# Ten instead of seven up-projection pairs in seven products, three in a row with a plain one between; half of a low part by VectorE where two of them meet

## The chip, the cores and the metric

One core of a Trainium2 chip runs the whole layer in one launch. The metric is the device time of one execution in microseconds. The kernel before takes 816.15 us (median of 3 runs, 815.88 to 816.3).

## The reference

One layer of a bidirectional encoder over 512 tokens of width 1024: attention and a gated scan side by side, cross-attention into 256 memory rows, and a gated MLP with a depthwise convolution of three taps between the up-projection and the activation. The change is in the MLP (and one copy in the scan).

```python
def conv_ffn(h, w_up, conv_w, conv_b, w_down):        # h 512 x 1024, w_up 1024 x 5632
    u = h @ w_up
    half = CONV_W // 2                                # CONV_W = 3
    up = jnp.pad(u, ((0, 0), (half, half), (0, 0)))
    acc = conv_b
    for j in range(CONV_W):
        acc = acc + up[:, j:j + n] * conv_w[j]
    gate, val = jnp.split(acc, 2, axis=-1)            # 2816 columns each
    return (jax.nn.silu(gate) * val) @ w_down

def reference(x, mem, ...):
    ...
    mixed = jnp.concatenate([att, rec], axis=-1) @ w_out[l]
    x = x + rmsnorm(mixed, post_mix_g[l])
    ...
    x = x + rmsnorm(memory_cross_attention(h, m, w_xq[l], w_xkv[l], w_xo[l]), post_x_g[l])
    h = rmsnorm(x, pre_ffn_g[l])
    x = x + rmsnorm(conv_ffn(h, w_up[l], conv_w[l], conv_b[l], w_down[l]), post_ffn_g[l])
    return x
```

## The kernel before, in words

**Arithmetic.** A float32 number is split into a high part and a low part (the number minus its high part), both in a rounded type that TensorE multiplies fast. Each product is three matmuls (`mm3`): high by high, high by low, low by high. On the page these are L278, L279 and L280. PE names the matmul, PEld the load of its stationary operand, which is here the block of weights. So L280's load needs the low part of the weights and the other two need the high part.

**Up-projections.** `w_up` is cut into 22 up-projections, i = 0 to 21, each with 128 columns of the gate and 128 of the value. An up-projection is done in one of two ways:

- *plain:* two units of weights, 1024 rows x 128 columns each, one for the gate and one for the value. A unit is laid out as 128 partitions x 1024 and takes 24 matmuls of 512 columns.
- *a pair in seven products* (`strassen_pair`, the i in `UP_S`): gate and value together, by Strassen's scheme in Winograd's form, with seven products of half size instead of eight. The products are w11, w22, t2, w21, t3, t1, t4 in this order, each with four steps of `mm3`, 84 matmuls of 256 columns in all. The weights are four units: **diag** (w11 and w22, from DRAM), **side** (t2 and w21, where w21 comes from DRAM and t2 is summed on the chip), **sums** (t3 and t1, a tile called "both") and **last** (t4, half the size). VectorE sums blocks for them in `add_blocks`: L197 writes "both" from the raw diag and the raw side, L200 writes t2 over the first half of the raw side, and the sum for t4 follows. Before the change the pairs are 6, 8, ..., 18, with a plain one between any two of them.

**A unit's way** (`issue`, called with three units in hand, `AHEAD`): SP loads the raw block from DRAM by DMA (L189, 512 KB). ACT casts the high part `wh` (L222). The low part `wl` is made in one of two ways. Either VectorE subtracts (L224), or ACT writes the negated high part into `wl` (L229) and a DMA from POOL's queue adds the weights from DRAM to it (L230). `LOW_FROM` says from which column on the second way is used: the diag wholly (512 KB by DMA), the side from column 512 on (256 KB; its first half isn't in DRAM), all others not at all. `wh` and `wl` have four buffers each, so a unit takes those of the unit four before it and waits until TensorE is done with them. The raw blocks have two rooms called "raw" and two called "tmp", in turn.

**Sums for the down-projection.** It uses the same scheme, with sums of blocks of `w_down` kept in DRAM. They are made beside the up-projections: a DMA from SP copies a block (a seed), and a DMA from POOL's queue adds another one (L251, an *add*, 512 KB; the last of each six has 256 KB). An add is issued behind a mark, a tiny copy on POOL (L236) that waits for the low part of the unit just issued. `adds_at` holds the units that are followed by an add. Each plain up-projection from 2 on gives one, and a second one only where no pair stands ahead of it.

**After the products** come the convolution (`conv`: one step on ACT, L1069, and two on VectorE, L1070, for each of gate and value), the activation, and the product of gate and value (L1083). For a pair, VectorE also joins the seven results out of PSUM (L1146 to L1155). Each engine works off its own instructions in order; how the four engines' instructions are interleaved in each queue is decided by a scheduler when the program is built, from the code's order and its data dependencies.

**The scan** (`hgrn_core`, four heads) copies two operands at L632, `kc` and `qc`. The copy of `qc` for head 1 is on VectorE and all others are on ACT.

Of the kernel before, what the change touches and what calls it, by code (L numbers as in the profile page):

```python
# [20 lines left out]
T = 512  # L21
# [4 lines left out]
FF = 2816  # L26
NF = FF // P
EPS = 1e-6
UP_S = (6, 8, 10, 12, 14, 16, 18)
N_MIX, N_WHOLE = 66, 110 - 2 * len(UP_S)  # L30
N_DOWN = N_WHOLE + 4 * len(UP_S)
N_UNITS = N_DOWN + 42
# [5 lines left out]
UP_PRODUCTS = (("w11", 0), ("w22", 1), ("t2", 0), ("w21", 1), ("t3", 1), ("t1", 0), ("t4", 0))  # L38
LAY_AHEAD, LOAD_AHEAD = 3, (7, 5)
SIDES_AT = (19, 20)  # L40
LOW_FROM = {"diag": 0, "side": 512}
SEEDS_AT = frozenset(range(28, 46)) | frozenset(range(60, 66))
ADDS_AT = frozenset(range(56, 62))
NEG_GROUP = frozenset((p, 1) for p in (2, 5, 6))
# [3 lines left out]
NEG_SCALAR = frozenset(range(9, 33))  # L48
NEG_POOL = frozenset(range(33, 42))
# [9 lines left out]
def pat(t, off, dims):  # L59
    a = t[:]  # L60
    return bass.AP(tensor=a.tensor, offset=a.offset + off, ap=[list(a.ap[0])] + [list(d) for d in dims])
# [28 lines left out]
def layer(tc, io, out):  # L90
    nc = tc.nc
# [16 lines left out]
    def bank(tag):  # L108
        return ps.tile([P, 512], F32, name="ps_" + tag, tag=tag)
# [35 lines left out]
    plan = [("w", i) for i in range(N_MIX)]  # L145
    whole, adds_at = N_MIX, set(ADDS_AT)
    for i in range(NF):
        if i in UP_S:
            plan += [(kind, UP_S.index(i)) for kind in ("diag", "side", "sums", "last")]
        else:  # L150
            if i >= 2:
                adds_at.update((len(plan), len(plan) + (i - 1 not in UP_S)))
            plan += [("w", whole), ("w", whole + 1)]
            whole += 2
    assert len(plan) == N_DOWN and whole == N_WHOLE
# [16 lines left out]
    def source(i):  # L172
        kind, n = plan[i]
        return io["w"][n] if kind == "w" else io["wu"][n, ("diag", "side").index(kind)]

    def load_w():
        i = loaded[0]
        loaded[0] += 1
        if i >= N_DOWN:
            p, u = divmod(i - N_DOWN, 6)  # L180
            cols = width(u)
            raw = raw_room(i)[:, :cols.stop - cols.start]
            src = weight_block(PRODUCTS[p][0], cols)
        else:
            if plan[i][0] in ("sums", "last"):
                return None
            raw = raw_room(i)
            src = source(i)
        last_load[0] = nc.sync.dma_start(raw, src).ins  # L189
        return raw  # L190

    def add_blocks(kind, raw, ahead):
        if kind == "diag":
            both = vp.tile([P, 1024], F32, name="both", tag="vv")
            mid = ahead[:, :512]
            with tc.issue_after(last_low[0]):
                nc.vector.tensor_tensor(out=both.rearrange("p (a n) -> p a n", a=2),  # L197
                                        in0=raw.rearrange("p (a n) -> p a n", a=2),
                                        in1=mid[:, None, :].to_broadcast([P, 2, 512]), op=ALU.add)
            nc.vector.tensor_add(mid, both[:, :512], raw[:, half(1)])  # L200
            pair_sums["sums"] = both
        elif kind == "side":
            pair_sums["last"] = tmp2(tag="tq")
            nc.vector.tensor_add(pair_sums["last"], raw[:, :512], raw[:, half(1)])
# [3 lines left out]
    def issue():  # L208
        i = issued[0]
        issued[0] += 1  # L210
        raw = raws.popleft() if raws else load_w()
        kind = plan[i][0] if i < N_DOWN else "w"
        if kind == "diag" and not raws:
            raws.append(load_w())
        if raw is None:
            raw = pair_sums[kind]
        wh = wp.tile([P, 1024], F32R, name="wh", tag="wh")
        wl = wp.tile([P, 1024], F32R, name="wl", tag="wl")
        if raw.shape[1] < 1024:
            wh, wl = wh[:, :raw.shape[1]], wl[:, :raw.shape[1]]  # L220
        by_dma = 0 if i in NEG_SCALAR or i in NEG_POOL else LOW_FROM.get(kind, raw.shape[1])
        nc.scalar.copy(wh, raw)  # L222
        if by_dma:
            last_low[0] = nc.vector.tensor_sub(wl[:, :by_dma], raw[:, :by_dma], wh[:, :by_dma].bitcast(F32)).ins  # L224
        if by_dma < raw.shape[1]:
            if i in NEG_POOL:
                nc.gpsimd.tensor_scalar(wl, wh.bitcast(F32), -1.0, 0.0, op0=ALU.mult, op1=ALU.add)
            else:
                nc.scalar.mul(wl[:, by_dma:], wh[:, by_dma:].bitcast(F32), -1.0)  # L229
            nc.gpsimd.dma_start(wl[:, by_dma:], source(i)[:, by_dma:], accum_op=ALU.add)  # L230
        add_blocks(kind, raw, raws[0] if raws else None)
        pending.append((wh, wl))
        if i in SEEDS_AT:
            seeds.popleft()()
        if i in adds_at and adds:
            with tc.issue_after(nc.gpsimd.tensor_copy(mark, wl[:, 0:1].bitcast(F32)).ins):  # L236
                adds.popleft()()
# [22 lines left out]
    def issue_ahead():  # L260
        while issued[0] < min(hold[0], taken[0] + AHEAD):
            issue()
        while N_MIX + 4 <= taken[0] and loaded[0] < min(N_UNITS, taken[0] + LOAD_AHEAD[loaded[0] >= N_DOWN]):
            raws.append(load_w())
# [189 lines left out]
    raw = rawp.tile([P, 1024], F32, name="raw", tag="raw")  # L454
# [163 lines left out]
    def hgrn_core(h):  # L618
        while h not in heads:
            yield None  # L620
        q, qk, tt = heads[h]
# [4 lines left out]
        diag = a[:, :, 0, :]  # L626
# [2 lines left out]
        nc.vector.scalar_tensor_tensor(out=ksum, in0=qk[:, 1, 1, :], scalar=oml[:, 1, h:h + 1], in1=ksum,  # L629
                                       op0=ALU.mult, op1=ALU.add)  # L630
        for side, to in ((1, kc), (0, qc)):
            (nc.vector.tensor_copy if (h, side) == (1, 0) else nc.scalar.copy)(  # L632
                to, pat(qk, side * 2 * T, [[2, T // 2], [T + 1, 2]]))
        o = bank("c").rearrange("p (b n) -> p b n", b=NB)
        for b in range(NB):
            nc.tensor.matmul(o[:, b, :], ksum[:, blk(b)], q[:, blk(b)], start=True, stop=True)
# [197 lines left out]
    def cores():  # L834
        for h in range(3):
            yield from hgrn_core(h)
# [94 lines left out]
    def attention_filler():  # L931
# [11 lines left out]
        kv["y0"] = yield from res_first(mix, MIX_ORDER, lambda j: rec_done[0] == 4 if j >= 2 else att_done[0] >= 2 * j + 2)  # L943

    weave((hgrn_core(3), 22.0), (attention(), 46.0), (attention_filler(), 52.0))

    x = load_x()
# [180 lines left out]
    def strassen_pair(i):  # L1128
        g, m, n = next_bank(), next_bank(), next_bank()
        place = {"w11": (g, near), "t2": (m, far), "t1": (m, near), "w22": (n, near), "t3": (n, far),  # L1130
                 "w21": (g, near), "t4": (g, far)}
        two, more, val = tmp2(tag="th"), tmp2(tag="th"), tmp2(tag="tq")
        for k, (name, at_w) in enumerate(UP_PRODUCTS):
            if k % 2 == 0:
                w = take()
            (hi, lo), cols = left_h[name]
            o, at = place[name]
            o = o[:, at]
            for kc in range(4):
                wc = slice(at_w * 512 + kc * P, at_w * 512 + kc * P + P)  # L1140
                mm3(o, (w[0][:, wc], w[1][:, wc]), (hi[:, kc, cols], lo[:, kc, cols]), kc == 0 and name != "w21",
                    kc == 3, name == "w21")
            if name == "w11":
                nc.scalar.copy(two[:, near], o)
            elif name == "t2":
                nc.vector.tensor_sub(two[:, far], o, two[:, near])  # L1146
            elif name == "t3":
                nc.vector.tensor_add(more[:, far], o, two[:, far])
            elif name == "t1":
                nc.vector.tensor_add(more[:, near], o, two[:, far])  # L1150
                nc.vector.tensor_tensor(out=val.rearrange("p (a t) -> p a t", a=2),
                                        in0=n.rearrange("p (a t) -> p a t", a=2),
                                        in1=more[:, None, near].to_broadcast([P, 2, 256]), op=ALU.add)
            elif name == "t4":
                nc.vector.tensor_sub(o, o, more[:, far])  # L1155
        conv(0, i, g)
        conv(1, i, val)

    for i in range(2, NF):
        if i in UP_S:  # L1160
            strassen_pair(i)
# [185 lines left out]
```

## Time and profile before

| what | value |
|---|---|
| runs, median (lowest to highest) | 816.15 us (815.88 to 816.3) |
| the profiled execution | 816.71 us |
| its span, first to last instruction | 813.8 us |
| granted TensorE clock, mean | 0.998 |
| up-projections in pairs, plain | 7, 15 |
| L222, casts of weights (ACT) | 110, 113.7 us |
| L224, low parts by VectorE | 77, 92.3 us |

The span is shorter than the time because the time also has the start and the end of the program. In the views below a row of a timeline is start, duration (us), engine, line, operation and tiles, then the idle time ahead of it and what ended that. A row of the DMA view is tiles, queue, count, KB each and the median time from issue to landing. A row of windows is the stretch, its length, and for each engine the busy time and number of instructions, then the clock, the busy share of the DMA engines and GB/s.

### The profile page before, as it was taken

To read this page: it belongs to the slowest core of one execution; us is meant where nothing else is said; L and a number is where in the kernel's file an instruction comes from. 1 tells how busy PE (TensorE), PEld (TensorE's weight loads), DVE (VectorE), ACT (ScalarE), POOL (GpSimd) and SP (SyncE) were. 2 spreads that over 40 slices of the span, in tenths; PEclk is the share of its full clock that TensorE was granted. 3 is DMA by queue.
4 is the path that set the end of the run, shared out by engine and by line. 5 is a ranking of instruction groups with operands and counts; after the bars stand their busy time and mean duration, and the time that the engine had idled before them with its cause. 6 is when DMAs were issued, how large, how long until landed. Compare 5 with 4: busy or idle time off the path is not lost.

```text
span 813.8 us, 11771 instructions
## 1 busy us (share of the span) xinstructions
PE 803.3 (99%) x4426; PEld 691.0 (85%) x4426; DVE 574.7 (71%) x868; ACT 482.1 (59%) x796; POOL 136.9 (17%) x213
## 2 busy tenths in 40 slices
PE   9999999999999999999999999999999999999996
PEld 7888888889998887888888898899999998888885
DVE  5456587469886865855453767987777788888765
ACT  5675757459988874644543553665555545566651
POOL 0111201053233102301010311211111111000301
PEclk9999999999999999999999999999999999999999
DMA  8685645569899753256634158776665677278852
GB/s 296 202 259 139 160 103 117 118 159 247 229 250 254 182 172 126 78 181 157 180 117 142 33 164 208 154 200 166 179 171 143 150 200 178 91 208 278 239 130 104
DMA packets 42457, 139.61 MB, mean 172 GB/s; under 512 B 5280, under 2 KB 6560, under 8 KB 42400
## 3 DMA queue, kind: packets, MB, share of 16 engines
q1 hardware_dynamic: 28944, 97.43, 35.5%
q0 software_dynamic: 12160, 38.54, 26.2%
q10 hardware_dynamic: 1296, 2.89, 1.0%
q8 instruction: 34, 0.56, 0.3%
q14 instruction: 23, 0.19, 0.1%
HBM read 135.17 MB, written 25.17 MB: 197 GB/s over the span
## 4 chain that ended last, share of the span: by engine, by line
PE 92%; DVE 3%; ACT 2%; issue 1%; POOL 1%; DMA 0%; DVEq 0%; POOLq 0%; SPq 0%; ACTq 0%
PE ps_b L279 10%; PE ps_b L280 10%; PE ps_b L278 10%; PE ps_s L278 6%; PE ps_s L280 6%; PE ps_s L279 6%; PE ps_o L278 5%; PE ps_o L279 5%; PE ps_o L280 5%; PE ps_c L278 5%; PE ps_c L280 5%; PE ps_c L279 5%; PE ps_c L647 3%; PE ps_o L893 2%; PE ps_s L872 2%; PE ps_o L882 2%
## 5 line engine op out<-in xcount | busy, mean ns | idle before, releaser
L222 ACT CAST wh<-raw 128x1024 fp32r<-128x1024 f32 x110 | 113.7, 1035 | 114.6 <-PE ps_b L279 35.3
L224 DVE TENSOR_TENSOR wl<-raw,wh 128x1024 fp32r<-128x1024 f32 (+1 forms) x77 | 92.3, 1201 | 72.2 <-ACT wh L222 72.0
L278 PE MATMUL ps_b<-big,wh 128*128 128x512 f32 (+1 forms) x344 | 122.3, 355 | 0.0
L280 PE MATMUL ps_b<-big,wl 128*128 128x512 f32 (+1 forms) x344 | 121.2, 352 | 0.0
L279 PE MATMUL ps_b<-big,wh 128*128 128x512 f32 (+1 forms) x344 | 121.2, 352 | 0.0
L280 PEld LDWEIGHTS ps_b<-big,wl 128*128 128x128 f32 x344 | 65.1, 189 | 8.5 <-DMA wl<-in_wu_dram 0.2
L278 PEld LDWEIGHTS ps_b<-big,wh 128*128 128x128 f32 x344 | 65.1, 189 | 8.3
L279 PEld LDWEIGHTS ps_b<-big,wh 128*128 128x128 f32 x344 | 65.1, 189 | 8.1
L673 DVE TENSOR_TENSOR big<-big 128x512 f32<-128x512 f32 x64 | 47.2, 755 | 9.6 <-PE ps_c L647 4.0
L278 PE MATMUL ps_s<-wh,big 128*128 128x512 f32 (+1 forms) x140 | 53.4, 383 | 0.0
L279 PE MATMUL ps_s<-wl,big 128*128 128x512 f32 (+1 forms) x140 | 53.3, 381 | 0.0
L280 PE MATMUL ps_s<-wh,big 128*128 128x512 f32 (+1 forms) x140 | 53.0, 379 | 0.0
L230 POOL DMA_DIRECT2D wl<-in_w_dram x33 | 29.3, 887 | 126.7 <-ACT wl L229 91.5
L122 DVE TENSOR_TENSOR big<-ps_o,big 128x512 fp32r<-128x512 f32 x54 | 36.9, 687 | 15.0 <-ACT big L121 13.4
L121 ACT CAST big<-ps_o 128x512 fp32r<-128x512 f32 x54 | 31.7, 588 | 18.5 <-PE ps_o L996 7.5
L278 PE MATMUL ps_s<-big,wh 128*128 128x256 f32 (+1 forms) x120 | 40.0, 334 | 0.0
L279 PE MATMUL ps_s<-big,wh 128*128 128x256 f32 (+1 forms) x120 | 40.0, 333 | 0.0
L280 PE MATMUL ps_s<-big,wl 128*128 128x256 f32 (+1 forms) x120 | 40.0, 333 | 0.0
L278 PE MATMUL ps_o<-wh,big 128*128 128x512 f32 (+1 forms) x102 | 39.2, 385 | 0.0
L279 PE MATMUL ps_c<-big,wh 128*128 128x256 f32 (+1 forms) x120 | 39.1, 326 | 0.0
L278 PE MATMUL ps_c<-big,wh 128*128 128x256 f32 (+1 forms) x120 | 39.1, 326 | 0.0
L280 PE MATMUL ps_c<-big,wl 128*128 128x256 f32 (+1 forms) x120 | 39.1, 326 | 0.0
(315 smaller groups left out, 2149.3 us busy)
## 6 DMA issues: line engine op xcount, KB each, us to landing
raw<-in_w_dram SPq DMA_DIRECT2D x91, 512.0 KB, 3.6
wl<-in_w_dram POOLq DMA_DIRECT2D x33, 512.0 KB, 7.3
sum_t<-in_wd_dram SPq DMA_DIRECT2D x20, 512.0 KB, 6.3
tmp<-in_wu_dram SPq DMA_DIRECT2D x14, 512.0 KB, 6.9
sum_t<-in_wd_dram POOLq DMA_DIRECT2D x10, 512.0 KB, 8.4
sum_t<-sum_t POOLq DMA_DIRECT2D x10, 512.0 KB, 7.5
big<-sum_t SPq DMA_DIRECT2D x10, 512.0 KB, 4.7
raw<-sum_t SPq DMA_DIRECT2D x10, 512.0 KB, 4.4
```

What stands on the lines that cost most here:

```text
L121: nc.scalar.copy(hi, src)
L122: (eng or nc.vector).tensor_sub(lo, src, hi.bitcast(F32))
L222: nc.scalar.copy(wh, raw)
L224: last_low[0] = nc.vector.tensor_sub(wl[:, :by_dma], raw[:, :by_dma], wh[:, :by_dma].bitcast(F32)).ins
L230: nc.gpsimd.dma_start(wl[:, by_dma:], source(i)[:, by_dma:], accum_op=ALU.add)
L278: nc.tensor.matmul(o, a[0], b[0], start=start, stop=False, skip_group_check=again)
L279: nc.tensor.matmul(o, a[0], b[1], start=False, stop=False, skip_group_check=again)
L280: last_mm[0] = nc.tensor.matmul(o, a[1], b[0], start=False, stop=stop, skip_group_check=again).ins
L647: nc.tensor.matmul(o[:, b, :], kc[:, blk(b)], qc[:, blk(b)] if m == 1 else pat(qk, b * P, [[2 * m, P // (2 * m)], [T + m, 2], [1, m]]), st ...
L673: nc.vector.tensor_tensor(out=c, in0=c, in1=pat(tt, toff + off, [[2, npair], [gap, 2], [0, m]]), op=ALU.mult)
L872: nc.tensor.matmul(s, qT[h // 4][:, h % 4, blk(qb)], kT[:, 2 * (h // 4) + c, :], start=c == 0, stop=c == 1)
L882: nc.tensor.transpose(o[:, c, :], e[:, 0, blk(c)], ident)
```

## The change

`UP_S` gets three more pairs, 9, 13 and 17, so that the pairs are 6, then three groups of three in a row (8, 9, 10; 12, 13, 14; 16, 17, 18), with plain 7, 11 and 15 ahead of the groups. Where a pair directly follows a pair (`close`), the first half of its diag's low part is made by VectorE and only the second half by ACT and the DMA of POOL. Every plain up-projection from 2 on is followed by two adds. The copy of `qc` for head 1 goes to ACT. Lines 222 to about 632 move down by one.

```diff
-UP_S = (6, 8, 10, 12, 14, 16, 18)
+UP_S = (6, 8, 9, 10, 12, 13, 14, 16, 17, 18)
...
-LOW_FROM = {"diag": 0, "side": 512}
+LOW_FROM = {"diag": 0, "next": 512, "side": 512}
...
-                adds_at.update((len(plan), len(plan) + (i - 1 not in UP_S)))
+                adds_at.update((len(plan), len(plan) + 1))
...
-        by_dma = 0 if i in NEG_SCALAR or i in NEG_POOL else LOW_FROM.get(kind, raw.shape[1])
+        close = kind == "diag" and UP_S[plan[i][1]] - 1 in UP_S
+        by_dma = 0 if i in NEG_SCALAR or i in NEG_POOL else LOW_FROM.get("next" if close else kind, raw.shape[1])
...
-            (nc.vector.tensor_copy if (h, side) == (1, 0) else nc.scalar.copy)(
-                to, pat(qk, side * 2 * T, [[2, T // 2], [T + 1, 2]]))
+            nc.scalar.copy(to, pat(qk, side * 2 * T, [[2, T // 2], [T + 1, 2]]))
```

How this moves instructions is shown at three places; the numbers behind a name count tiles and differ between the two programs.

**ACT, where the diag and the side of a pair are made.** Before, these are the units of pair 10, made while plain 9 runs; the cast of `tmp4_5306` is that of the side:

```order
L222 CAST wh_5395<-tmp4_5265 128x1024
L229 ACTIVATE wl_5396<-wh_5395 128x1024
L222 CAST wh_5431<-tmp4_5306 128x1024
L1069 ACTIVATE tmp2_5418<-ps_s_5296,cw_303 128x512
L1069 ACTIVATE tmp2_5423<-tmp2_5301,cw_303 128x512
L229 ACTIVATE wl_5432<-wh_5431 128x512
```

After the change, the units of pair 10 (the third of the group 8, 9, 10) are made while pair 9 runs:

```order
L223 CAST wh_5468<-tmp4_5340 128x1024
L230 ACTIVATE wl_5469<-wh_5468 128x512
L1075 ACTIVATE tmp2_5421<-tmp2_5421 128x512
L223 CAST wh_5504<-tmp4_5375 128x1024
L223 CAST wh_5541<-both_5474 128x1024
L230 ACTIVATE wl_5505<-wh_5504 128x512
L223 CAST wh_5576<-tmp2_5510 128x512
```

The diag's negation has half its length, and the cast of "both" (the unit of sums) now stands between the cast of the side and the side's negation, so that the negation starts only after it.

**PE, the end of a pair.** Before, in pair 8, product t3 (bank `ps_o`, weights `wh_5261`) is followed by t1 (`ps_c`, the same weights), four steps each, and then by t4 (`wh_5302`); one step of t1 and one of t4 stand here for four alike:

```order
L278 MATMUL ps_c_5297<-big_4768,wh_5261 128x256
L279 MATMUL ps_c_5297<-big_4768,wh_5261 128x256
L280 MATMUL ps_c_5297<-big_4768,wl_5262 128x256
...
L278 MATMUL ps_s_5296<-big_4239,wh_5302 128x256
L279 MATMUL ps_s_5296<-big_4241,wh_5302 128x256
L280 MATMUL ps_s_5296<-big_4239,wl_5303 128x256
```

After the change, in pair 9, two of the four steps of t4 (bank `ps_b`, weights `wh_5439`) come between t3 (`ps_c`) and t1 (`ps_s`, weights `wh_5404`), and the other two behind t1:

```order
L281 MATMUL ps_c_5435<-big_4770,wl_5405 128x256
L279 MATMUL ps_b_5433<-big_4239,wh_5439 128x256
L280 MATMUL ps_b_5433<-big_4241,wh_5439 128x256
L281 MATMUL ps_b_5433<-big_4239,wl_5440 128x256
...
L279 MATMUL ps_s_5434<-big_4768,wh_5404 128x256
L280 MATMUL ps_s_5434<-big_4768,wh_5404 128x256
L281 MATMUL ps_s_5434<-big_4768,wl_5405 128x256
...
L281 MATMUL ps_b_5433<-big_4239,wl_5440 128x256
```

So the buffers of the sums (`wh_5404`, `wl_5405`) come free six matmuls later within the pair.

**POOL, from plain 7 to the DMAs of the pair behind it.** Before:

```order
L236 COPY mark_88<-wl_5126 128x1
L251 DMA sum_t2_2_2916<-sum_t1_2_1917 128x1024
L230 DMA wl_5188<-in_wu_dram 128x1024
L230 DMA wl_5222<-in_wu_dram 128x512
```

After the change:

```order
L237 COPY mark_88<-wl_5126 128x1
L252 DMA sum_t2_2_2916<-sum_t1_2_1917 128x1024
L237 COPY mark_88<-wl_5157 128x1
L252 DMA sum_t2_3_3028<-sum_t1_3_1976 128x1024
L231 DMA wl_5190<-in_wu_dram 128x1024
L231 DMA wl_5224<-in_wu_dram 128x512
L231 DMA wl_5332<-in_wu_dram 128x512
L231 DMA wl_5368<-in_wu_dram 128x512
```

A second mark and a second add stand ahead of the 512 KB of the diag of pair 8; behind them come the side of pair 8 and the half diag and the side of pair 9, 256 KB each.

## The prediction

> **What bounds the kernel now.** I read the page's busy shares and its chain first, then the windows of the up-projection, then the waits of the weight loads there.
>
> ```profile
> PE 803.3 (99%) x4426; PEld 691.0 (85%) x4426; DVE 574.7 (71%) x868; ACT 482.1 (59%) x796; POOL 136.9 (17%) x213
> ...
> PE 92%; DVE 3%; ACT 2%; issue 1%; POOL 1%; DMA 0%; DVEq 0%; POOLq 0%; SPq 0%; ACTq 0%
> ...
> 554.06:564.14 10.08, 10.08 (x86) 10.07 (x85) 7.60 (x11) 5.03 (x7) 1.02 (x2) 1.00 0.35 84
> 564.14:575.04 10.90, 10.90 (x50) 9.02 (x49) 8.58 (x13) 6.68 (x10) 2.84 (x4) 1.00 1.02 261
> ...
> PEld ps_b L280 <- DMA wl<-in_wu_dram: 0.2, 1, 0.2
> ```
>
> TensorE is busy 99% of the span and 92% of the chain, so the time is the sum of its matmuls plus the little it waits. The two rows of windows are one pair in seven products (up-projection 8) and the plain one after it (9). Their columns are the stretch, its length, then busy time of PE, PEld, DVE, ACT, POOL. PE has no gap in either, and the clock column is 1.00. The last row is the only wait for an operand that the weight loads have from 470 to 705 us: 0.2 us for a low part that a DMA finishes. So matmuls taken out there shorten the kernel one for one, unless the weights come later than TensorE wants them.
>
> **Term 1, the matmuls.** Three up-projections (9, 13, 17) go from 48 matmuls of 512 columns in 10.90 us to 84 of 256 columns in 10.08 us. 3 x (10.90 - 10.08) = **2.46 us less**. The number of 512 KB loads stays, two for a plain up-projection and two for a pair; the pair adds low parts by DMA, which is term 2.
>
> [...]
>
> **Term 2, when the low parts land.** A unit's wh and wl take the buffers of the unit four before it. Within a group each unit's buffers are freed by the same unit of the pair before, so it has 7.2 us of matmuls ahead of it (three of its four units; 8.64 us for the last) instead of 11 to 14 us. For half of a diag or a side block the path is: TensorE frees the buffers, ACT casts wh, ACT writes -wh into half of wl, POOL issues the accumulating DMA, it lands, PEld may load.
>
> ```profile
> 541.48 0.28 PE L279 MATMUL ps_s<-big,wh 128*128 128x256 f32 x1
> ...
> 541.80 1.05 ACT L222 CAST wh<-tmp 128x1024 fp32r<-128x1024 f32 x1 [1.83 <-PE ps_s L279]
> 542.93 1.06 ACT L229 ACTIVATE wl<-wh 128x1024 fp32r<-128x1024 f32 x1
> 543.89 1.03 ACT L222 CAST wh<-tmp 128x1024 fp32r<-128x1024 f32 x1
> 544.83 0.78 ACT L1069 ACTIVATE tmp<-ps_b,cw 128x512 f32<-128x512 f32 x1
> ...
> 546.21 0.62 ACT L229 ACTIVATE wl<-wh 128x512 fp32r<-128x512 f32 x1
> ...
> 547.12 0.85 POOL L230 DMA_DIRECT2D wl<-in_wu_dram  x1 [1.97 <-ACT wl L229]
> ...
> 529.99 0.88 POOL L230 DMA_DIRECT2D wl<-in_wu_dram  x1 [4.33 <-ACT wl L229]
> ...
> wl<-in_wu_dram POOLq DMA_DIRECT2D x1, 256.0 KB, 7.5
> ...
> 537.54 0.39 PE L280 MATMUL ps_b<-big,wl 128*128 128x256 f32 x1
> ```
>
> From these rows: ACT starts 0.32 us after the start of the releasing matmul (541.48 to 541.80); cast to its own negation is 1.13 (541.80 to 542.93); cast to another instruction behind it 0.94 (543.89 to 544.83); start of the negation to the DMA's issue 0.91 (546.21 to 547.12); and TensorE goes on 0.05 after landing (529.99 + 7.5 = 537.49, then 537.54; the DMA row is the issue at 529.99). Let L be the time from issue to landing of 256 KB, and 0 the start of a group's first pair, so that the second starts at 10.08 and the third at 20.16.
>
> The **third pair's side block** is the tight one. In the order of ACT its negation stands behind the cast of "both". That cast waits for the second pair's sums to be used up, which in the new order of PE is the 77th matmul of the pair, since half of "last" is put ahead of it: 10.08 + 76 x 0.12 = 19.20, cast 19.52, negation 20.46, issue 21.37, landing 21.37 + L. Product w21 reads this half with the third matmul of its first step, the 39th of the pair: 20.16 + 38 x 0.12 = 24.72. Wait = 21.37 + L + 0.05 - 24.72 = **L - 3.30**.
>
> The others have more room by the same steps. Second pair's diag: its cast is at 2.98, issue 5.02, needed at 11.76, room for L up to 6.7. Third pair's diag: cast about 13.2, issue 15.3, needed at 21.84, room 6.5. Second pair's side: its first half is the sum that VectorE writes over the raw block (L200), and this sets its cast.
>
> ```profile
> 556.94 0.69 DVE L1083 TENSOR_TENSOR big<-tmp,tmp 128x512 f32<-128x512 f32 x1
> 558.10 1.23 DVE L224 TENSOR_TENSOR wl<-raw,wh 128x1024 fp32r<-128x1024 f32 x1 [0.46 <-ACT wh L222]
> ...
> 562.45 1.22 DVE L197 TENSOR_TENSOR both<-tmp,tmp 128x1024 f32<-128x1024 f32 x1
> 563.59 0.42 DVE L1150 TENSOR_TENSOR tmp<-ps_c,tmp 128x256 f32<-128x256 f32 x1
> 563.92 0.68 DVE L200 TENSOR_TENSOR tmp<-both,tmp 128x512 f32<-128x512 f32 x1
> 564.52 0.69 DVE L1151 TENSOR_TENSOR tmp<-ps_o,tmp 128x512 f32<-128x512 f32 x1
> ...
> 566.65 0.75 DVE L1070 SCALAR_TENSOR_TENSOR tmp<-ps_s,cw,tmp 128x511 f32<-128x511 f32 x1
> 567.32 0.75 DVE L1070 SCALAR_TENSOR_TENSOR tmp<-tmp,cw,tmp 128x511 f32<-128x511 f32 x1
> ```
>
> Start to start, VectorE takes 1.13 for a block of 1024, 0.33 for 256 columns from PSUM, 0.60 for 512 and 0.67 for a convolution step. Second pair: the diag's half low part starts at 4.06 (558.10 - 554.06 = 4.04, after the cast), "both" 4.66, L1146 5.79, L200 6.12 to 6.81; ACT casts the side at 6.87, negates at 8.00, issue 8.91, needed at 14.64, room for L up to 5.7. Third pair: from the first pair's last product (ready at 8.84) VectorE runs with hardly a gap, L1150 and L1151 to 9.90, low part of "both" 11.04, L1155 and the low part of "last" 11.97, 0.34 for ACT's convolution step, four steps 14.99, half of the diag 15.59, the product L1083 16.36, "both" 17.49, L1146 17.83, L200 to 18.51. ACT casts the side at 18.55 to 19.49, just ahead of the 19.52 above: this chain does not add to the wait, but it has no slack.
>
> **What L is.** No transfer of 256 KB into wl ran alone. The nearest rows:
>
> ```profile
> q1 hardware_dynamic: 28944, 97.43, 35.5%
> q0 software_dynamic: 12160, 38.54, 26.2%
> ...
> wl<-in_w_dram POOLq DMA_DIRECT2D x1, 512.0 KB, 5.2
> ...
> raw<-in_w_dram SPq DMA_DIRECT2D x1, 512.0 KB, 3.3
> sum_t<-sum_t POOLq DMA_DIRECT2D x1, 256.0 KB, 5.2
> ...
> wl<-in_wu_dram POOLq DMA_DIRECT2D x1, 256.0 KB, 7.7
> ```
>
> 512 KB accumulated into wl with almost no other traffic (issue at 148.61) took 5.2. The queue rows give the cost of the bytes: 26.2% of 813.8 us for 38.54 MB is 1.45 us for 256 KB, so alone it should take 5.2 - 1.45 = 3.75. A 512 KB load costs 35.5% x 813.8 x 0.524 / 97.43 = 1.55 us, and one goes out at about 20.7, the next pair's side block, as soon as VectorE is done with its room (the half low part of the third side); a part of it lies under this DMA: plus 0.5, **L = 4.3**, an estimate. The ends: a plain load alone took 3.3; 256 KB behind a 512 KB accumulate and with three loads took 7.7. In a group the traffic is thinner than in that row, 256 KB at a time some 3 to 6 us apart, and the sums of the down weights are added only in plain ones; so I stay near 5.2, the row of the same kind and alone. Wait 1.0 us in each of three groups: **3.0 us more**. At the ends: 3.3 gives no wait. 7.7 gives 2.0 at the second side and 4.4 at the third, 6.4 a group, 19.2.
>
> **Small terms.** The copy of one operand of head 1 goes from VectorE to ACT.
>
> ```profile
> 100.61 0.50 DVE L632 COPY tmp<-big 128x512 f32<-128x512 f32 x1
> 101.04 2.15 DVE L673 TENSOR_TENSOR big<-big 128x512 f32<-128x512 f32 x2
> ...
> 103.33 0.84 PE L647 MATMUL ps_c<-big,tmp 128*128 128x128 f32 x5 [0.72 <-DVE big L673]
> ```
>
> TensorE waits there for L673, which also needs the other copy, on ACT until 101.0, so it starts no earlier. ACT would finish the moved copy at about 101.8, after the 101.25 at which TensorE used it, but inside the wait that ends at 103.33. I take 0; between a gain of one matmul put ahead (0.2) and a loss of 0.5.
>
> **Term 3, the second add ahead of a group.** Plain 7, 11 and 15 stand between pairs and now add two low-part sums of the down weights by DMA instead of one. The second is issued once VectorE has written the low part of the plain one's second unit, and so stands in POOL's queue ahead of the next group's first diag, 512 KB.
>
> ```profile
> 539.37 0.84 POOL L251 DMA_DIRECT2D sum_t<-sum_t  x1 [0.30 <-issue]
> 544.28 0.88 POOL L230 DMA_DIRECT2D wl<-in_wu_dram  x1 [4.07 <-ACT wl L229]
> ...
> 540.00 1.23 DVE L224 TENSOR_TENSOR wl<-raw,wh 128x1024 fp32r<-128x1024 f32 x1 [0.92 <-ACT wh L222]
> ...
> wl<-in_wu_dram POOLq DMA_DIRECT2D x1, 512.0 KB, 8.9
> ...
> wl<-in_wu_dram POOLq DMA_DIRECT2D x1, 512.0 KB, 8.7
> ...
> 554.06 0.28 PE L278 MATMUL ps_s<-big,wh 128*128 128x256 f32 x1
> ...
> 541.00:554.00 13.00, 13.00 (x68) 11.15 (x67) 10.74 (x17) 7.94 (x10) 1.73 (x2) 1.00 0.95 235
> ```
>
> With plain 7 as it was, the add goes out at 539.37 and the diag at 544.28; that lands 8.9 later, 553.2 (the 8.9 row), and its first use is the third matmul of the pair, 554.06 + 0.24 = 554.30: 1.1 us to spare. The second add would go out about 541.85, after the low part that ends at 541.23. The DMA engines are busy 0.95 of 541 to 554 (the column after the clock), so only 13 x 0.05 = 0.65 us is idle there, and 512 KB of this queue cost 2.9 us (twice the 1.45 above): the diag lands 2.9 - 0.65 to 2.9 later and TensorE waits 1.15 to 1.8. Ahead of 12 the second add is the last of its sum, of 256 KB: 1.45 - 0.65 - 1.1 is below nothing, 0 to 0.35. The other end is 0 for all three: in the cycle whose add had 256 KB instead of 512 (issue 601.91) the diag took 8.7 instead of 8.9, so half an add made 0.2 of difference, not 1.45. The saturated engines are the nearer row, and I take 1.3, 0.3 and 1.3: **2.9 us more**, between 0 and 4.0.
>
> **Sum.** -2.46 + 3.0 + 2.9 + 0 = +3.4. The profiled execution took 816.71 us (span 813.84), which becomes 820.1; the median of the runs, 816.15, is 0.56 below it and becomes **819.6**.
>
> **Rivals.** [...] If L is 3.3 or less and the second add delays the diag by 1.1 or less, nothing waits: 816.15 - 2.46 = 813.7; it is faster by more than 0.2% as long as all six waits are under 0.8 together. For it: TensorE waited for such a DMA only once before, 0.2 us, the loads alone take 3.3, and half an add made 0.2. Against it: 5.2 alone for 512 KB, and the 0.95. [...] Chance 0.18.
>
> *Only one of the two waits comes:* L = 4.3 with the add hidden, or the add's 2.9 with L at 3.3: 816.6 to 816.7. Chance 0.15.
>
> *The transfers are slowed inside the group as before:* at the third side each 1 us of L costs 3 us, and from 5.7 the second side waits too. L = 5.5 gives 3 x 2.2 = 6.6 for term 2: 823.2, or 824.3 with term 3 at its top; 7.7 gives 835.8. For it: all seven rows of this DMA had 6.7 to 7.7. Against it: they all shared the queue with a 512 KB accumulate. Chance 0.13.
>
> *VectorE becomes the bound in a group.* It is busy 16.2 of the 21 us of the two windows. A plain one needs two low parts of 1.2, four steps of 0.75 and a product of 0.69, 6.1 in all, so a pair needs about 10.1, and 0.6 more where half the low part is added: 10.7 against 10.08. Being 0.6 late in each of two pairs delays the side's cast by up to 0.6, three times: 819.6 + 1.8 = 821.4. Against it: the walk above ends in time, and the plain one behind the group has 4.8 us free. Chance 0.06.
>
> *It does not do what it says:* the two windows repeat to 0.01 us over the pairs before, so I leave 0.02 for a pair not being 0.82 shorter.
>
> **Numbers.** The forecast keeps 0.46; with L from 3.9 to 4.8 (1.8 to 4.5) and term 3 from 1.5 to 4.0 it spans 817.0 to 822.2. A measurement of this kernel can tell about 0.2%, 1.6 us, from no change. Faster is below 814.5: 0.16 of the first rival. Slower is above 817.8: 0.38 of the forecast, 0.13 of the third rival, 0.06 of the fourth, 0.01 of the fifth, 0.58. The rest is 0.26. The range takes in the first rival's 813.7 and ends at 824.3, above which L and the add would both stand at their tops.
>
> **What would show it.** In the profile after: a pair in a group shows 10.08 us in its windows apart from its waits; about 1 us of the weight load at L281 waiting for the DMA into wl at the start of pairs 8 and 16, less at 12; about 1 us in the middle of each third pair (10, 14, 18), and none or nearly none in the second; 256 KB landing in about 4.3 us; the cast of the third side right before that of "both". Wrong if the waits fall at the second side or at first halves (VectorE), if a group's first diag lands in 9 as before, or if 256 KB land in 3.3 or in 7.

## The result, and the profile after

The changed kernel takes 827.67 us (median of 4 runs, 824.71 to 831.0) against 816.22 before: 1.014 times as long, 95% interval 1.0123 to 1.0158. The forecast was 819.6, with a range that ended at 824.3. The direction is right, the size is not: 11.5 us more instead of 3.4. The profiled execution took 824.71 us (span 822.9), the shortest of the four; 8.0 above the profiled one of before.

The page's busy times and the chain of the changed kernel:

```profile
PE 803.8 (98%) x4534; PEld 695.2 (84%) x4534; DVE 590.8 (72%) x900; ACT 490.6 (60%) x812; POOL 142.2 (17%) x219
...
PE 81%; DMA 8%; DVE 5%; ACT 3%; issue 2%; POOL 1%; POOLq 0%; DVEq 0%; ACTq 0%
```

A DMA, which had 0% of the chain before, has 8%. The timeline of the weight loads shows where. These are all its waits for this DMA; the number in brackets is the wait. They come in threes: the start of a group (pairs 8, 12, 16), the side of the second pair (9, 13, 17), and the side of the third (10, 14, 18).

```profile
555.38 0.19 PEld L281 LDWEIGHTS ps_s<-big,wl 128*128 128x128 f32 x1 [1.18 <-DMA wl<-in_wu_dram]
570.64 0.19 PEld L281 LDWEIGHTS ps_b<-big,wl 128*128 128x128 f32 x1 [0.81 <-DMA wl<-in_wu_dram]
582.44 0.19 PEld L281 LDWEIGHTS ps_o<-big,wl 128*128 128x128 f32 x1 [1.66 <-DMA wl<-in_wu_dram]
600.79 0.19 PEld L281 LDWEIGHTS ps_b<-big,wl 128*128 128x128 f32 x1 [1.64 <-DMA wl<-in_wu_dram]
615.87 0.19 PEld L281 LDWEIGHTS ps_o<-big,wl 128*128 128x128 f32 x1 [0.63 <-DMA wl<-in_wu_dram]
627.38 0.19 PEld L281 LDWEIGHTS ps_c<-big,wl 128*128 128x128 f32 x1 [1.39 <-DMA wl<-in_wu_dram]
645.41 0.19 PEld L281 LDWEIGHTS ps_o<-big,wl 128*128 128x128 f32 x1 [1.31 <-DMA wl<-in_wu_dram]
660.32 0.19 PEld L281 LDWEIGHTS ps_c<-big,wl 128*128 128x128 f32 x1 [0.47 <-DMA wl<-in_wu_dram]
671.99 0.19 PEld L281 LDWEIGHTS ps_s<-big,wl 128*128 128x128 f32 x1 [1.53 <-DMA wl<-in_wu_dram]
```

4.1 at the starts, 1.9 at the second sides, 4.6 at the third: 10.6 us. With the 2.46 that the matmuls give back, 816.71 - 2.46 + 10.6 = 824.9, and 824.71 was measured: in this execution the waits are everything. The DMA view shows what each waited for. First the diag of pair 8 (issue at 544.23), then in the first group, from 562 to 578, the second side (564.13) with the loads from SP beside it, and the third side (577.50):

```profile
wl<-in_wu_dram POOLq DMA_DIRECT2D x1, 512.0 KB, 11.1
...
raw<-in_w_dram SPq DMA_DIRECT2D x2, 512.0 KB, 5.6
...
wl<-in_wu_dram POOLq DMA_DIRECT2D x1, 256.0 KB, 6.5
...
wl<-in_wu_dram POOLq DMA_DIRECT2D x1, 256.0 KB, 4.9
```

The diag lands after 11.1 us instead of 8.9, the second side after 6.5 and the third after 4.9. The forecast had taken 4.3 for both sides.

### The profile page after: what moved, and what is told of

Read it like the earlier page. It is cut to its first block, busy times and chain, and to the rows that moved or that the text cites. A ratio compares the mean times of both kernels' runs of the same rounds, so it can differ in the third digit from the quotient of the medians.

```text
span 822.9 us, 12049 instructions
## 1 busy us (share of the span) xinstructions
PE 803.8 (98%) x4534; PEld 695.2 (84%) x4534; DVE 590.8 (72%) x900; ACT 490.6 (60%) x812; POOL 142.2 (17%) x219
## 4 chain that ended last, share of the span: by engine, by line
PE 81%; DMA 8%; DVE 5%; ACT 3%; issue 2%; POOL 1%; POOLq 0%; DVEq 0%; ACTq 0%
PE ps_b L281 9%; PE ps_b L280 9%; PE ps_b L279 9%; DMA wl<-in_wu_dram 8%; PE ps_s L281 6%; PE ps_s L280 5%; PE ps_s L279 5%; PE ps_o L281 4%; PE ps_o L279 4%; PE ps_o L280 4%; PE ps_c L281 3%; PE ps_c L280 3%; PE ps_c L279 3%; PE ps_c L647 3%; PE ps_o L893 2%; PE ps_s L872 2%
## 5 line engine op out<-in xcount | busy, mean ns | idle before, releaser
L225 DVE TENSOR_TENSOR wl<-raw,wh 128x1024 fp32r<-128x1024 f32 (+1 forms) x77 | 89.1, 1159 | 66.1 <-ACT wh L223 65.6
L281 PE MATMUL ps_b<-big,wl 128*128 128x512 f32 (+1 forms) x356 | 123.0, 346 | 2.0 <-DMA wl<-in_wu_dram 2.0
L279 PE MATMUL ps_b<-big,wh 128*128 128x512 f32 (+1 forms) x356 | 124.1, 349 | 0.0
L280 PE MATMUL ps_b<-big,wh 128*128 128x512 f32 (+1 forms) x356 | 122.7, 345 | 0.0
L281 PEld LDWEIGHTS ps_b<-big,wl 128*128 128x128 f32 x356 | 67.4, 189 | 10.1 <-DMA wl<-in_wu_dram 2.4
L280 PEld LDWEIGHTS ps_b<-big,wh 128*128 128x128 f32 x356 | 67.5, 190 | 7.6
L279 PEld LDWEIGHTS ps_b<-big,wh 128*128 128x128 f32 x356 | 67.5, 190 | 7.5
L281 PE MATMUL ps_o<-big,wl 128*128 128x256 f32 (+1 forms) x124 | 39.7, 320 | 3.0 <-DMA wl<-in_wu_dram 3.0
L230 ACT ACTIVATE wl<-wh 128x1024 fp32r<-128x1024 f32 (+1 forms) x44 | 39.7, 903 | 1.8 <-PE ps_c L281 0.5
L279 PE MATMUL ps_o<-big,wh 128*128 128x256 f32 (+1 forms) x124 | 39.4, 318 | 0.0
```

Of the source, the lines that this page charges most:

```text
L279: nc.tensor.matmul(o, a[0], b[0], start=start, stop=False, skip_group_check=again)
L280: nc.tensor.matmul(o, a[0], b[1], start=False, stop=False, skip_group_check=again)
L281: last_mm[0] = nc.tensor.matmul(o, a[1], b[0], start=False, stop=stop, skip_group_check=again).ins
```

## The experiments

Each is one edit of the changed kernel, if not said otherwise. Each ran beside the kernel before on the same chip, whose median there was 816.14 for e0 to e3, 816.34 for e4 to e7, 815.9 for e8 to e10 and 816.42 for e11.

### e0, without an edit

> The changed kernel once more, without an edit. Its profile showed nine waits of the weight loads at L281 for the DMA into wl, 10.6 us in all: 4.1 at the starts of the groups, 1.9 at the side of each second pair, 4.6 at the side of each third one. Waits theory (the low parts land late, nothing else): the nine waits come again within 0.3 us each and the profiled execution is again about 8 us above that of before. Rival (something else that varies, such as the granted clock): the median stands about 11 us above before, 3 more than the waits explain, and where a run is longer its clock is lower.

827.56 us (826.76 to 828.91), 1.013 (1.0109 to 1.0151). So the median, some 11 us above before, is the kernel's own, and the first profile was a short one. The profiled execution took 828.91, and its waits aren't the same: 1.73 at the start of pair 8, none at 12, 2.74 at 16, and 11.5 in all. The windows after three of them (the clock stands behind POOL's busy time) show what else it lost:

```profile
556.40:558.00 1.60, 1.60 (x13) 1.60 (x14) 1.53 (x3) 0.15 (x1) 0.00 (x0) 1.00 0.45 96
583.40:585.00 1.60, 1.59 (x8) 1.59 (x9) 1.60 (x3) 0.00 (x0) 0.51 (x1) 0.57 0.02 8
585.00:587.00 2.00, 2.00 (x11) 2.00 (x11) 0.46 (x2) 1.04 (x1) 0.86 (x1) 0.50 0.72 262
587.00:589.00 2.00, 2.00 (x19) 2.00 (x18) 2.00 (x3) 0.00 (x0) 0.76 (x3) 0.99 0.88 86
...
648.70:650.00 1.30, 1.30 (x8) 1.30 (x7) 0.00 (x0) 0.37 (x1) 0.00 (x0) 0.50 0.01 2
650.00:652.00 2.00, 2.00 (x12) 2.00 (x11) 0.00 (x0) 0.04 (x1) 0.00 (x0) 0.52 0.00 0
652.00:656.00 4.00, 4.00 (x36) 4.00 (x36) 2.92 (x5) 1.76 (x3) 0.85 (x1) 1.00 0.13 18
```

After the wait of 1.73 the clock stays at 1.00. After the one of 2.06 (ended at 583.41) and the one of 2.74 (647.70) TensorE runs at about half of it for some 3.4 us each, which loses 1.7 us each. 816.14 - 2.46 + 11.5 + 3.4 = 828.6, and 828.91 was measured. The rival of the expectation, a varying clock, holds beside the waits: the clock fell to 0.50 right after two of them.

### e1, the second add one unit earlier

```diff
-                adds_at.update((len(plan), len(plan) + 1))
+                adds_at.update((len(plan), len(plan) + (-1 if i - 1 in UP_S else 1)))
```

> The changed kernel, but the two adds at plain 7, 11, 15 and 19 are issued behind the pair's last unit and the plain one's first unit, one unit earlier than in the change. Queue theory (the second add, ahead of the diag in POOL's queue, delays it on saturated engines): the diags of pairs 8, 12, 16 land 1 to 3 us earlier, the waits at the starts of the groups fall from 4.1 us to 0.5 or less, the other six stay; about 3.6 to 4 us faster than the changed kernel. Rival (the loads, not the add, delay the diag): it lands as late as before, no change.

820.57 us, 7.0 under e0; 1.0049 (1.003 to 1.0069) of before. The diags of 8, 12 and 16 land after 8.7, 7.8 and 9.4 us instead of 11.1, 11.2 and 10.8, and no start of a group waits. The six other waits stay, 6.1 us together, none over 1.5, and no stretch is at half clock. So the second add is what delays the diag, and the gain is more than the 4.1 us of waits at the starts. In the profile of e0 these waits were 4.5 us, and half clock took 3.4 more, half of it after one of them and half after a wait at a third side.

### e2, the third side negated before "both" is cast

```diff
-        nc.scalar.copy(wh, raw)
+        if kind == "sums":
+            with tc.issue_after(last_neg[0]):
+                nc.scalar.copy(wh, raw)
+        else:
+            nc.scalar.copy(wh, raw)
...
-                nc.scalar.mul(wl[:, by_dma:], wh[:, by_dma:].bitcast(F32), -1.0)
+                last_neg[0] = nc.scalar.mul(wl[:, by_dma:], wh[:, by_dma:].bitcast(F32), -1.0).ins
```

> The changed kernel, but on ACT the negation of a third pair's side stands ahead of the cast of both instead of behind it. Order theory: the DMA of the third side is issued 0.94 us earlier in each group, the waits there fall from 4.6 to about 1.8 us, 2.8 us faster. Rival (VectorE's sum sets the time of the side, not the cast): the issue moves less than 0.3 and so does the time.

829.97 us: not 2.8 faster but 2.4 slower than e0. The third sides did more than was expected: their waits fell from 4.6 to 0.85 in all, not 1.8, since two of the three DMAs also landed sooner, after 4.2 us. But the starts of the next groups wait 3.00 and 3.73 us, since their diags now take 12.5 and 13.3 us to land, and TensorE then runs at half clock (0.50). The timeline of the weight loads at the start of pair 16:

```profile
649.69 0.28 PEld L286 LDWEIGHTS ps_o<-big,wl 128*128 128x128 f32 x1 [3.73 <-DMA wl<-in_wu_dram]
```

and the windows after it, with the clock at 0.50:

```profile
649.69:652.00 2.31, 2.31 (x11) 2.31 (x12) 0.00 (x0) 0.00 (x0) 0.00 (x0) 0.50 0.11 20
652.00:654.00 2.00, 2.00 (x11) 2.00 (x11) 0.00 (x0) 0.37 (x1) 0.00 (x0) 0.50 0.00 0
654.00:658.00 4.00, 4.00 (x31) 4.00 (x31) 2.35 (x4) 1.68 (x2) 0.86 (x1) 0.85 0.00 0
```

As I read it, the waits inside a group had given the transfers before the next one time, and once taken away they came back there, all at once and with the clock on top. At pair 16 the diag lands 16.9 us after the first add of plain 15 (15.9 in the first profile), but TensorE needs it 13.2 us after that add instead of 14.7.

### e3, the next load held back until the side has landed

```diff
             nc.gpsimd.dma_start(wl[:, by_dma:], source(i)[:, by_dma:], accum_op=ALU.add)
+            if kind == "side" and UP_S[plan[i][1]] - 1 in UP_S:
+                nc.gpsimd.tensor_tensor(out=mark, in0=wl[:, 1023:1024].bitcast(F32), in1=raw[:, 1023:1024], op=ALU.add)
```

> The changed kernel, but the room of the raw side of each second and third pair is held until the DMA of its low part has landed (a tiny sum on POOL reads both), so that the next 512 KB load is not beside this DMA. Traffic theory (256 KB take 6.3 us at the second side and 4.8 at the third because loads lie beside them): they land in about 4.9 and 4.0, the waits at the second side go from 1.9 to 0 and at the third from 4.6 to about 2.3, 4.2 us faster. Rival (the accumulating DMA has this latency by itself): no change, or slower where POOL's queue is blocked.

827.59 us, as e0. The traffic theory itself is confirmed: in the first group the second side lands after 4.5 us instead of 6.5 and the third after 3.7 instead of 4.9 (two rows of the DMA view, issued at 564.35 and 576.86; in the other groups 4.7 and 5.8, and 3.7 twice):

```profile
wl<-in_wu_dram POOLq DMA_DIRECT2D x1, 256.0 KB, 4.5
...
wl<-in_wu_dram POOLq DMA_DIRECT2D x1, 256.0 KB, 3.7
```

The second sides no longer wait, and the third ones wait 0.5 each. But the starts of 12 and 16 wait as in e2, and the gain is gone. The timeline of the weight loads there:

```profile
600.49 0.19 PEld L283 LDWEIGHTS ps_b<-big,wl 128*128 128x128 f32 x1 [3.15 <-DMA wl<-in_wu_dram]
...
647.45 0.29 PEld L283 LDWEIGHTS ps_o<-big,wl 128*128 128x128 f32 x1 [3.77 <-DMA wl<-in_wu_dram]
```

### e4, the edits of e1 and e2 together

> The early adds of e1 and the earlier negation of e2 together. In e2 the saved waits at the third sides came back at the next group's start, where two adds, four loads and the diag's DMA follow each other on busy DMA engines. Theory (the start of a group is bound by these bytes; e1 took the second add out of the way): the third sides' waits fall from 4.1 (e1) to about 1.3 us, at most 1 us comes back at pair 16, whose diag landed in e1 just when it was needed; no wait over 2 us, no stretch at half clock; about 2.5 us under e1, 818. Rival (what is saved inside the group is given back at the next start whatever the order of the adds): as e1, 820.5, or above it.

817.69 us, 1.0016 (1.0003 to 1.003). Only the second sides wait: 0.7, 0.7 and 0.6, as the waits of the weight loads by bank show.

```profile
PEld ps_b L286 <- DMA wl<-in_wu_dram: 0.9, 2, 0.7
PEld ps_o L286 <- DMA wl<-in_wu_dram: 0.7, 1, 0.7
PEld ps_c L286 <- DMA wl<-in_wu_dram: 0.6, 1, 0.6
```

(The first row has 0.2 at pair 6, which was there before.) The same edit that lost 2.4 us alone (e2) is worth 2.9 once the second add is out of the way. The profiled execution took 816.07: 816.71 - 2.46 + 2.0 = 816.25, so the matmuls gave back what the prediction said.

### e5, e4 with the load held at the second side alone

The edit of e3 with `and UP_S[plan[i][1]] + 1 in UP_S` in its condition.

> As e4, and the room of the raw side of each second pair is held until the DMA of its low part has landed, so that only one 512 KB load lies beside it. Theory: the second sides' 2.0 us of waits in e1 go too, 816 or just under, no clear difference from before; with no wait at all it would be 813.7. Rival (given back at the next start): 818 or more.

821.62 us (817.91 to 826.0), 3.9 above e4. The second sides wait no more, but the third ones do, 1.3, 1.6 and 1.3. The timeline of VectorE and ACT ahead of the first third side shows one reason:

```profile
567.58 0.74 DVE L1079 SCALAR_TENSOR_TENSOR tmp<-ps_s,cw,tmp 128x511 f32<-128x511 f32 x1
568.24 0.74 DVE L1079 SCALAR_TENSOR_TENSOR tmp<-tmp,cw,tmp 128x511 f32<-128x511 f32 x1
568.89 0.68 DVE L230 TENSOR_TENSOR wl<-tmp,wh 128x512 fp32r<-128x512 f32 x1
569.50 0.68 DVE L1090 TENSOR_TENSOR big<-tmp,tmp 128x512 f32<-128x512 f32 x1
570.10 1.22 DVE L198 TENSOR_TENSOR both<-tmp,tmp 128x1024 f32<-128x1024 f32 x1
571.24 0.41 DVE L1153 TENSOR_TENSOR tmp<-ps_s,tmp 128x256 f32<-128x256 f32 x1
571.57 0.68 DVE L201 TENSOR_TENSOR tmp<-both,tmp 128x512 f32<-128x512 f32 x1
...
572.33 1.05 ACT L228 CAST wh<-tmp 128x1024 fp32r<-128x1024 f32 x1 [3.06 <-PE ps_c L288]
```

VectorE has no gap, and the cast (572.33) starts 0.08 after its sum over the side ends (571.57 + 0.68 = 572.25). The row names a matmul as what ended the wait, but by the times it was the sum. With TensorE on time, VectorE sets when the side is cast. The other reason is the landing: the DMA issued at 574.39 met a load at 574.58 and took 5.5 us instead of the 4.6 of e4 (5.7 and 5.5 instead of 4.2 in the other groups). e5 does not separate the two. In its three slowest executions, 823.75 to 826.0, the granted clock was 0.992 to 0.993, against 0.997 in the profiled one of 817.91.

### e6, two adds at each plain one, without groups

The changed kernel with `UP_S` of before; the copy of head 1 is on ACT.

> The kernel before with two parts of the change alone: two adds at each plain one, and the copy of head 1 on ACT; the seven pairs as before. Pairs 8, 12 and 14 get a diag behind two adds of 512 KB, 10 and 16 behind 512 and 256 KB. Queue theory: each such diag lands 1.5 to 2.9 us later than before and TensorE waits 0.5 to 1.5 us at the starts of 8, 12 and 14 and 0 to 0.7 at 10 and 16; 2 to 5 us slower than before, 818 to 821. Rival (only with groups is there a wait): same as before.

820.52 us, 1.0053 (1.0039 to 1.0068). The starts of pairs 8, 12 and 14 wait 1.2, 1.5 and 1.1 us, those of 10 and 16 not at all:

```profile
PEld ps_b L281 <- DMA wl<-in_wu_dram: 1.5, 2, 1.1
PEld ps_o L281 <- DMA wl<-in_wu_dram: 1.5, 1, 1.5
PEld ps_s L281 <- DMA wl<-in_wu_dram: 1.2, 1, 1.2
```

(0.4 of the first row is pair 6.) The diags of 8, 12 and 14 land after 11.1, 11.4 and 11.0 us, that of 10, behind one add of 512 and one of 256 KB, after 9.8. So term 3 of the prediction holds by itself, with its size.

### e7, the close diag wholly by DMA

```diff
-LOW_FROM = {"diag": 0, "next": 512, "side": 512}
+LOW_FROM = {"diag": 0, "next": 0, "side": 512}
```

> The changed kernel, but the low part of a close diag is made wholly by ACT and the DMA, 512 KB, as before; VectorE has no half of it. DMA theory: the second and third diags land in 5.5 to 6.5 us, still in time, but the second side's DMA stands behind 1.45 us more and its waits grow from 1.9 to about 5 us in all; 2 to 4 us slower than the changed kernel. VectorE rival (VectorE is what makes the sides late): the sides are cast 0.6 us earlier and it is faster.

835.32 us, 7.8 above e0, more than twice what was expected. Neither theory has it right: no side waits any more. The close diags do, each at the third matmul of its pair: 1.4, 0 and 0.6 us in the second pairs, 3.2, 0.7 and 2.6 in the third. The diag of pair 10, 512 KB issued at 573.48, and the weight load that waits for it:

```profile
wl<-in_wu_dram POOLq DMA_DIRECT2D x1, 512.0 KB, 8.0
...
581.54 0.29 PEld L281 LDWEIGHTS ps_o<-big,wl 128*128 128x128 f32 x1 [3.17 <-DMA wl<-in_wu_dram]
```

With half the bytes, the same diag landed after 4.1 us in the first profile, and no close diag waited. The starts wait 1.8, 3.0 and 2.9, and half clock (0.50) follows three of the waits. The half by VectorE is worth having: in this kernel, moving it back to POOL's queue costs 7.8 us in all.

### e8, e4 with VectorE's sums ahead of the low part

```diff
+        if close:
+            add_blocks(kind, raw, raws[0], True)
+            with tc.issue_after(last_sum[0]):
+                last_low[0] = nc.vector.tensor_sub(wl[:, :by_dma], raw[:, :by_dma], wh[:, :by_dma].bitcast(F32)).ins
-        if by_dma:
+        elif by_dma:
```

(`add_blocks` sets `last_sum` to the sum over the side and is not called again for a close diag.)

> As e4, and on VectorE the sums of a close diag (both, and t2 over the side) stand ahead of the half of its low part, not behind it. In e5 the cast of the third side waited for VectorE's sum, after a stretch in which VectorE had no gap. VectorE theory (0.6 us of VectorE ahead of the sum are what holds the sides): the second and third sides are cast 0.6 us earlier, the second sides' waits (1.9 us in e4) fall to 0.5 or less, the profiled execution is 814 to 815 and the median 1 to 2 us under e4. Rival (only the DMA's landing counts): as e4 within 0.5.

818.57 us, 1.0029 (1.0018 to 1.004): a miss, no better than e4. The second sides wait no more. But earlier sums free the raw rooms earlier, so both of the next pair's loads lie beside the third side's DMA (issue at 573.03, loads at 572.22 and 573.75): it takes 7.4 us, and the third sides wait 1.3, 1.0 and 0.9, the starts of 12 and 16 0.4 and 0.9.

### e9, e4 with the half low part by POOL

```diff
-            last_low[0] = nc.vector.tensor_sub(wl[:, :by_dma], raw[:, :by_dma], wh[:, :by_dma].bitcast(F32)).ins
+            if close:
+                nc.gpsimd.tensor_sub(wl[:, :by_dma], raw[:, :by_dma], wh[:, :by_dma].bitcast(F32))
+            else:
+                last_low[0] = nc.vector.tensor_sub(wl[:, :by_dma], raw[:, :by_dma], wh[:, :by_dma].bitcast(F32)).ins
```

> As e4, and the half of a close diag's low part that VectorE makes is made by POOL instead, so that VectorE has 0.6 us less to do in each close pair. VectorE theory: as e8, second sides' waits 0.5 or less in all three groups, median 1 to 2 us under e4. Rival (POOL, slower at it, is late itself or holds up its own queue, in which the DMA of the same diag stands): waits appear at the diags of the second and third pairs and it is slower than e4.

816.19 us, 1.0001 (0.9991 to 1.001), 1.5 under e4. POOL takes 1.3 to 1.4 us for a half, where VectorE took 0.68, and its own DMA follows at once. The group of these instructions (busy us, mean ns of one):

```profile
L231 POOL TENSOR_TENSOR wl<-tmp,wh 128x512 fp32r<-128x512 f32 x3 | 4.2, 1390 | 16.7 <-ACT wh L228 16.7
```

One wait is left in the waits of the weight loads, at the first group's third side, whose DMA took 7.5 us:

```profile
PEld ps_o L289 <- DMA wl<-in_wu_dram: 1.5, 1, 1.5
```

### e10, the copy of head 1 alone

The kernel before with `nc.scalar.copy` for both operands.

> The kernel before with the copy of head 1 on ACT alone; pairs and adds as before. Theory: 0, at most 0.2 us faster (pair 6 began 0.2 us earlier in the changed kernel than before). Rival: a loss of 0.5.

816.54 us, 1.0002 (0.9994 to 1.0011): nothing, as forecast.

### e11, e9 with the load held at the third side

The edit of e3 in e9 with the condition `UP_S[plan[i][1]] - 1 in UP_S and UP_S[plan[i][1]] + 1 not in UP_S`.

> As e9, and the room of the raw side of each third pair is held until the DMA of its low part has landed, so that the second of the next pair's two loads is not beside it (in e9 it was, at 573.75, and the DMA took 7.5 us in the first group, the one wait left in its profile, 1.4 us). Traffic theory: that DMA lands in about 5 us, no wait over 0.3 us is left in the groups, the profiled execution is 814 to 815.5 and the median 0.5 to 1.5 us under e9 and under before. Rival (the loads held back come together with the next adds and make a group's start late): waits at the diags of 12 and 16, no gain over e9.

815.52 us (814.26 to 817.65), 0.9989 (0.9979 to 1.0). The DMA that took 7.5 us in e9 takes 3.7 (row of the DMA view, issued at 574.10):

```profile
wl<-in_wu_dram POOLq DMA_DIRECT2D x1, 256.0 KB, 3.7
```

No start and no side in the groups waits; the only wait of the weight loads for this DMA is at pair 6, which is outside them:

```profile
PEld ps_b L291 <- DMA wl<-in_wu_dram: 1.1, 1, 1.1
```

This is the only version whose median is under that of before, by 0.9 us, and its interval just reaches 1.0, so it is not clearly faster. With no wait at all it would be 816.42 - 2.46 = 814.0; the lowest of its 12 runs was 814.26.

## Why the prediction was wrong

**What bounds the kernel, and term 1,** hold. Where the waits are small the rest comes out: 816.25 worked out and 816.07 measured in e4.

**Term 2, the mechanism, holds to 0.1 us.** Its equation for the third side, wait = L - 3.30, with 0.12 us for a matmul of 256 columns (10.08 / 84), gives 1.6 for the 4.9 that was measured, and 1.66 was the wait. Its room of 5.7 for the second side gives 0.8 for 6.5, and 0.81 was the wait. It is as close for the other four sides of this profile and the six of e0. The order of ACT has the part in it that the prediction gave it: e2, which changes that order, took 3.75 of 4.6 us away at the third sides.

**The step that failed first is L,** "traffic in a group is thinner", so 4.3 for 256 KB. I gave the third side one load beside it and the second side none. In the trace two loads of 512 KB go out at 562.11 and 563.92, as VectorE frees the raw rooms of pair 9, around the second side's DMA at 564.13, and it takes 6.1 to 6.5 us in the three groups; the third side's takes 4.6 to 4.9. With the next load held back they take 4.5 to 5.8 and 3.7 (e3). Term 2 was 6.5 us and not 3.0. The rooms' release was there to be worked out with the same steps that gave the casts. The prediction took a wait at the second side for a sign of VectorE; here the load goes on at 570.64, right as that DMA lands (564.13 + 6.5 = 570.6).

**Term 3 is right in cause, and its size at two of three places:** 1.2 and 1.3 us at pairs 8 and 16, where I took 1.3; e1 and e6 show the second add as the cause. At pair 12, where I took 0.3, the first profile has 1.64 and that of e0 none. Ahead of 12 a copy of `post_ffn_g` (256 KB, 587.22 in the first profile) now lies between the adds and the diag, and I had left it out of the bytes: with it they are as many as ahead of 8 and 16, and the diag took 11.2 us as there. In all, term 3 was 4.1 us and not 2.9. In e0 the diag of 12 lands 15.3 us after the first of the two adds, 15.8 in the first profile; but TensorE, at half clock until 587.05, needs it only some 16.2 us after that add instead of 14.2. By these times the half clock is why nothing waits there; no run tests it.

**What the sum had no term for is the clock.** After nine of the ten waits beyond 2 us in the traces TensorE ran at half clock, 0.50 (last section). The first profile had none; in e0 it cost 3.4 us, and the median of after, 3 us above that profile, fits it. So the profiled execution passed its forecast, 820.1, by 4.6 us through terms 2 (3.5) and 3 (1.2), and the median is further off by about what the clock takes.

**The rivals.** "The transfers are slowed inside the group as before" came nearest, though the slowing is from the loads (with the next one held back, in e3, the second side takes 4.5 us instead of 6.5) and not from a 512 KB accumulate. The first rival, in which L is 3.3 or less and nothing waits, is refuted: the fastest 256 KB in the rows above took 3.7 us. "VectorE becomes the bound" shows only when other waits are gone, and in part: e8 and e9 both take 0.6 us of VectorE from ahead of the sums and both end the waits of the second sides, but only e9 is faster than e4, by 1.5 us; in e8 the third sides' DMAs slowed to 7.0 to 7.4 in all groups, in e9 in one.

## What to carry to other kernels

Work out for each transfer that something waits for which others are on the engines at that moment, from the instruction that frees each one's room, and not from the mean traffic of the stretch. Saved waits may come back at the next place that the same transfers feed (e2, e3): clear the place that is full of bytes first, then the smaller ones. And TensorE may come back from a wait slower than it went: here, after nine of the ten waits beyond 2 us, the clock was 0.50.

## What the runs showed of the hardware

**Half clock after a wait.** In the traces kept of after and its variants, ten waits of the weight loads were longer than 2 us. After nine of them (e0: 2.06, 2.74; e2: 3.00, 3.73; e3: 3.15, 3.77; e7: 3.17, 3.04, 2.92) the clock went to 0.50 within 1.6 us before or behind the wait's end, for about 3 to 6 us of matmuls, in which a matmul of 256 columns took 0.21 instead of 0.12 us start to start (e2, 602.20 to 605.83). After the tenth, 2.65 in e7, and after all up to 1.81 (e7) it stayed at 1.00.

So the length of a wait alone does not tell the two apart. In e0 the clock changes at 583.64, 587.05, 648.49 and 651.90, which are 1, 18 and 1 times 3.41 us apart; in e7 the slow matmuls begin at 608.45 and end at 611.86, 3.41 later. Cut in steps of 3.41 us from these times, the rows around e0's wait of 2.06 and then around e7's of 2.65 are:

```profile
580.23:583.64 3.41, 1.55 (x14) 1.35 (x13) 3.38 (x5) 2.26 (x3) 0.00 (x0) 1.00 0.67 156
583.64:587.05 3.41, 3.41 (x18) 3.41 (x18) 1.87 (x4) 1.04 (x1) 1.37 (x2) 0.50 0.42 154
...
673.28:676.69 3.41, 2.37 (x20) 2.16 (x19) 2.40 (x5) 1.67 (x2) 0.59 (x1) 1.00 1.04 229
676.69:680.10 3.41, 2.01 (x16) 2.01 (x17) 0.89 (x2) 0.52 (x2) 0.00 (x0) 1.00 0.92 249
680.10:683.51 3.41, 3.41 (x31) 3.41 (x30) 2.84 (x5) 2.81 (x4) 0.00 (x0) 1.00 0.00 0
```

In e0 PE is idle for 1.86 us of one such stretch (3.41 - 1.55), and the next has half clock. In e7 the longer wait falls into two stretches, with 1.04 and 1.40 idle, and neither is followed by it. In the nine cases the stretch ahead had 1.86 to 2.55 us idle; without half clock the most in the up-projections was 1.61 (e7). That does not hold everywhere: near the end of e11 a stretch with 1.95 idle (805.14 to 808.56) left the clock at 1.00. No run varies the idle time by itself.
